# The MLPs of a two-layer diffusion backbone: chunks of 1024 in layer 0, seven quarter products with all weight sums on VectorE in layer 1

## The chip, the cores and the metric

The kernel runs on one core of one Trainium2 chip. TensorE multiplies matrices into PSUM (which this kernel uses as eight banks of 128 partitions by 512 fp32 columns), VectorE and ScalarE work element by element, GpSimd and SyncE here mostly issue transfers. The metric is the device time of one execution in microseconds; of the kernel before, three were timed.

## The reference, cut to what matters

Everything is fp32. There are two layers over 512 latent tokens and 256 context tokens, width 1024, hidden width of the MLP 4096. In layer 0 both token sets run through the MLP, in layer 1 only the latent tokens.

```python
def sq_relu_mlp(h, w1, w2):
    return jnp.square(jax.nn.relu(h @ w1)) @ w2

for l in range(DEPTH):                      # DEPTH = 2
    ...                                     # modulation, token mixer
    x = x + g1 * ox
    x = x + g2 * sq_relu_mlp(modulate(rmsnorm(x, norm_mlp[l]), sh2, sc2), w_ff1[l], w_ff2[l])
    if not last:
        h = h + cg1 * oc
        h = h + cg2 * sq_relu_mlp(modulate(rmsnorm(h, norm_mlp[l]), csh2, csc2), w_ff1[l], w_ff2[l])
return rmsnorm(x, norm_final)
```

The modulation (shift, scale, gate) comes from `silu(c) @ w_ada[l] + b_ada[l]`.

## The kernel before

Activations lie transposed: a tile holds 128 channels by the tokens (512 in layer 1, 512 + 256 = 768 in layer 0). Each fp32 operand is split into a rounded high part and the remainder, and each product of 128 x 128 weights is three matmuls (`mm3`: high x high, high x low, low x high). Weights arrive from HBM in tiles of up to 1024 columns (`load_unit`), and `split_piece` makes pieces of 512 columns out of them: ScalarE copies with rounding (`hi`, L219), VectorE subtracts (`lo`, L228).

The program is a list of tasks in order, one task about one output tile. `emit` walks through it; ahead of each task it splits weights up to AP_ = 4 pieces beyond the one needed, holds at most N_W = 6 split pieces, and loads units as long as at most N_R = 4 raw tiles are in use. `merge` mixes two lists in proportion to their costs. From this the recording layer makes one queue for each engine, which the engine works off in that order; an instruction that waits holds up what stands behind it on its engine.

Layer 0 MLP (`layer_ff` with `last` false): 8 chunks of 512 hidden channels. An "up" task makes a hidden tile in two halves of 384 tokens, each in a single PSUM bank; `evac` does the ReLU and the square on ScalarE and splits the result. Then eight "down" outputs (`plain`) sum over the chunk's four hidden tiles in a two-bank tile (512 + 256 columns), and VectorE adds them, times the gate, to x (`gate_update`, L1257). Between these tasks 96 tasks of row products for the modulation of layer 1 (L488, VectorE alone) are spread over the first seven chunks.

Layer 1 MLP (`last` true): 4 chunks of 1024. In the first three, the down product is taken as 2 x 2 blocks and computed with seven quarter products instead of eight (`block`, `product`): the weight quarters A11, A12, A22, A21 and their sums S1 to S4, against sums of the hidden tiles. S1 and S3 are formed by transfers: one brings a quarter twice (L240), another, issued by GpSimd, adds two further quarters to it (L244, accumulating). S2 and S4 are formed by VectorE (L264). Each product is 12 matmuls of 256 columns. What is shared between outputs is kept in tiles called V (`keep`, L1376, the first time copied by ScalarE, L1469), the rest goes straight to x (`gate`, L1461); `finish` combines the kept sums at the end. The fourth chunk is plain. All single banks are taken in a rotation over three two-bank tiles and two single banks (`bank`).

The last outputs of a layer run one token group after another (256 tokens each), so that the next norm (sum of squares, `norm_h` L565 to L569) can begin on the first groups.

Of the kernel before, what the change touches and what calls it, by code (L numbers as in the profile page):

```python
# [52 lines left out]
TAIL1 = 2  # L53
TL = False
# [8 lines left out]
N_RR = 2  # L63
# [27 lines left out]
class Unit:  # L91
# [4 lines left out]

    def __init__(self, ap, w, kind=None, queue=None):
        self.ap, self.w, self.kind, self.queue, self.plain = ap, w, kind, queue, False
# [49 lines left out]
class Net:  # L148
    def __init__(self, nc, tc, es, a):
# [9 lines left out]
        self.ps = self.half = None  # L159
        self.turn = 0  # L160
# [4 lines left out]
    def psum(self, na, nb):  # L165
# [4 lines left out]
        self.pa = self.ps.enter_context(self.tc.tile_pool(name=self.nm("pa"), bufs=na, space=PSUM))  # L170
# [499 lines left out]
    def layer_mix(self, l):  # L670
# [580 lines left out]
        out.append(Task(0, lambda: self.psum(3, 2)))  # L1251
# [9 lines left out]
    def residual_tasks(self, l, units, rhs, nk, chunk, whole, groups, tail, then=None):  # L1261
# [11 lines left out]
        def go(m, gs):  # L1273
            ps = self.A("res")
# [3 lines left out]
        def two(gs):  # L1278
            ps = [self.A("res"), self.A("res")]
# [52 lines left out]
    def layer_ff(self, l, whole, groups):  # L1332


# [4 lines left out]
        last = l == DEPTH - 1  # L1339
        w = NL if last else T  # L1340
        hw = w // 2
        MP = 1 if last else 2
        CP = 4 // MP
        n_chunk, n_blk = 16 // CP, 4 // MP
        halves = [[(0, 256, 0)], [(256, 256, 0)]] if last else [[(0, 384, 0)], [(384, 128, 0), (512, 256, 1)]]
        H = lambda k: self.h[k]
        out = []
        then = self.final_tasks(groups) if last else self.norm_tasks(l + 1, self.G1, 0, groups)
        B11, T1, B21, B22, T3, T2, T4 = range(7)
        act, st = {}, {}  # L1350
        per = T // hw
# [13 lines left out]
        def begin():  # L1365
            n = per * 2 // 4
            t = [self.d("V", F32).rearrange("p a t -> p (a t)") for _ in range(-(-3 // n))]
            for i, name in enumerate("U57"):
                st[name] = [t[i // n][:, (i % n * 4 + j) * hw:(i % n * 4 + j + 1) * hw] for j in range(4)]

        def negate():
            self.ng = self.sm.tile([P, 8, 2], F32, tag="ng", name=self.nm("ng"), bufs=1)
            w = 1 if last else 2
            nc.vector.tensor_scalar(self.ng[:, :, :w], self.mod[l][:, 40:48, :w], -1.0, None, op0=ALU.mult)
# [4 lines left out]
        def split_plain(c, m, half):  # L1379
            if (c, m) not in act:  # L1380
                t = self.d("act").rearrange("p a t -> p (a t)") if not last or m % 3 != 2 else None
                if not last:
                    act[c, m] = Halves(t[:, 0:T], t[:, T:2 * T])
                elif t is not None:
                    act[c, m] = Halves(t[:, 0:512], t[:, 512:1024])
                    act["spare", m] = t[:, 1024:1536]
                else:
                    act[c, m] = Halves(act.pop(("spare", m - 2)), act.pop(("spare", m - 1)))
            f = act[c, m]
            s = slice(0, w) if half is None else slice(half * hw, half * hw + hw)  # L1390
            b = st["b", m % 2][:, s]
            self.hi(f[:, 0, s], b)
            self.mark = self.lo(f[:, 1, s], b, f[:, 0, s])
# [22 lines left out]
        def evac(c, m, half, parts):  # L1416

            if half in (0, None):
                st["b", m % 2] = self.tmp("b")
            b = st["b", m % 2]  # L1420
            for ps, at, n in parts:
                nc.scalar.activation(b[:, at:at + n], ps, AF.Relu)  # L1422
            o, n = (0, w) if half is None else (half * hw, hw)
            nc.scalar.activation(b[:, o:o + n], b[:, o:o + n], AF.Square)
            if not last or c == n_chunk - 1:
                split_plain(c, m, half)
                return
            for i in (0, 1) if half is None else (half,):
                sums(c, m, i)

        def up(c, m, u):
            for half in (None,) if last else range(2):
                o, n = (half * hw, hw) if half is not None else (0, w)
                ps = self.bank("f1")
                for k in range(NK):
                    s = slice(k * P, (k + 1) * P)
                    self.mm3(ps[:, :n], u[:, 0, s], u[:, 1, s], H(k)[:, 0, o:o + n], H(k)[:, 1, o:o + n], k == 0, k == NK - 1)
                evac(c, m, half, [(ps[:, :n], o, n)])

        def up_two(us):  # L1440

            ps = [self.A("f1") for _ in us]
# [6 lines left out]
            for i in range(2):  # L1449
                for half in range(2):  # L1450
                    o = half * hw
                    evac(0, i, half, [(ps[i][:, o:o + hw], o, hw)])

        def gate(m, half, ps, neg=False):

            g = self.ng[:, m] if neg else self.mod[l][:, 40 + m]
            o = half * hw
            self.mark = None
            for at, n, cond in halves[half]:
                x = self.X(m)[:, at:at + n]  # L1460
                self.mark = nc.vector.scalar_tensor_tensor(x, ps[:, at - o:at - o + n], g[:, cond:cond + 1], x,  # L1461
# [292 lines left out]
```

## Time and profile before

| what | value |
|---|---|
| median of 3 runs | 1622.08 us (1621.45 to 1624.95) |
| the profiled execution | 1622.75 us, of which 1620.9 are its span |
| mean granted TensorE clock | 0.987 |
| TensorE (PE) busy | 1561.1 us, 96% of the span |
| weight loads (PEld) busy | 1334.8 us, 82%, beside PE |
| VectorE (DVE) busy | 1011.6 us, 62% |
| ScalarE (ACT) busy | 749.6 us, 46% |
| GpSimd (POOL) busy | 48.5 us, 3% |

The MLP of layer 0 runs from about 405 to 970 us, that of layer 1 from about 1250 us to the end. "Busy" says that an instruction was running; matmuls are pipelined and their ends are modelled. The granted clock is given as a share of 2.4 GHz. In a timeline, a number in brackets is the engine's idle time before that work, and behind the arrow stands what the profile takes to have ended it. In the chain of waits the last instruction of the program is followed back, step by step, to what released it.

### The profile page before, as it was taken

Reading aid. Unit: us, or ns where it says so; the run is one execution under the profiler, and the core shown is the slowest. Engines: PE = TensorE matmul, PEld = TensorE weight load, DVE = VectorE, ACT = ScalarE, POOL = GpSimd, SP = SyncE. Lnnn points to the kernel's source line nnn. Section 1 sums busy time; section 2 is a strip of 40 time slices with the busy share of each in tenths; the row PEclk is TensorE's granted clock in tenths of the full one; section 3 lists DMA queues with packets and bytes.
Section 4 is the critical chain, followed back from the end, with each engine's and each line's share of the span. In section 5 each row is a group of like instructions: output and inputs, shape, how many; then the busy total and the mean of one; then the engine's idle time right before and its main releaser. Section 6 shows DMA issues by size and latency. Waiting matters only on the chain.

```text
span 1620.9 us, 24503 instructions
## 1 busy us (share of the span) xinstructions
PE 1561.1 (96%) x9268; PEld 1334.8 (82%) x9268; DVE 1011.6 (62%) x2234; ACT 749.6 (46%) x1545; POOL 48.5 (3%) x90
## 2 busy tenths in 40 slices
PE   4999999999999999999999989999999999999997
PEld 2898657888889899898998988867888888888886
DVE  5665664886867655445454377686646775758734
ACT  4425466653524232242322454367754645445443
POOL 0110000000000000000000001101000000000000
PEclk8999999999999999999999999999999999999999
DMA  9352344554254334333333133524323354445421
GB/s 376 105 170 66 116 120 106 164 185 150 90 158 156 117 106 128 118 117 117 111 106 122 66 112 121 153 82 103 96 88 116 103 150 124 130 129 130 126 85 53
DMA packets 76966, 201.42 MB, mean 124 GB/s; under 512 B 9648, under 2 KB 12208, under 8 KB 76848
## 3 DMA queue, kind: packets, MB, share of 16 engines
q1 hardware_dynamic: 71728, 183.33, 36.0%
q0 software_dynamic: 4544, 16.00, 5.0%
q8 instruction: 73, 1.20, 0.3%
q10 hardware_dynamic: 576, 0.52, 0.1%
q14 instruction: 45, 0.37, 0.1%
HBM read 169.40 MB, written 10.49 MB: 111 GB/s over the span
## 4 chain that ended last, share of the span: by engine, by line
PE 88%; DVE 5%; DMA 4%; ACT 2%; issue 1%; SPq 0%; DVEq 0%; ACTq 0%
PE f L211 52%; PE A L211 10%; PE sc L211 4%; PE oe L211 3%; PE pv L211 3%; PE res L211 3%; PE rv L211 2%; PE pT L1045 2%; PE ada L211 2%; DMA sums<-w_ff 1%; PE ro L211 1%; PE q L211 1%; DMA raw<-w_ada 1%; PE rs L211 1%; DVE hn L565 1%
## 5 line engine op out<-in xcount | busy, mean ns | idle before, releaser
L211 PE MATMUL f<-h,wt 128*128 128x384 f32 (+2 forms) x2400 | 458.3, 351 | 2.6 <-ACT h L568 1.7
L211 PE MATMUL f<-act,wt 128*128 128x256 f32 (+1 forms) x2832 | 448.8, 319 | 7.0 <-DVE x L1461 4.4
L211 PEld LDWEIGHTS f<-h,wt 128*128 128x128 f32 x2400 | 412.5, 189 | 47.0 <-ACT b L1422 6.8
L211 PEld LDWEIGHTS f<-act,wt 128*128 128x128 f32 x2832 | 400.7, 190 | 53.5 <-DVE x L1461 5.2
L228 DVE TENSOR_TENSOR wt<-raw,wt 128x512 fp32r<-128x512 f32 (+1 forms) x320 | 218.5, 688 | 207.4 <-ACT wt L219 203.3
L219 ACT ACTIVATE wt<-raw 128x512 fp32r<-128x512 f32 (+1 forms) x320 | 199.2, 629 | 308.7 <-PE f L211 203.1
L211 PE MATMUL A<-h,wt 128*128 128x512 f32 (+2 forms) x864 | 172.3, 358 | 1.0 <-ACT h L568 0.5
L211 PEld LDWEIGHTS A<-h,wt 128*128 128x128 f32 x864 | 143.6, 191 | 27.3 <-ACT h L568 2.8
L1422 ACT ACTIVATE b<-f 128x384 f32<-128x384 f32 (+2 forms) x98 | 50.2, 518 | 158.2 <-PE f L211 158.1
L1257 DVE SCALAR_TENSOR_TENSOR x<-f,mod,x 128x256 f32<-128x256 f32 (+1 forms) x142 | 80.9, 602 | 55.4 <-PE f L211 55.4
L228 DVE TENSOR_TENSOR act<-b,act 128x384 fp32r<-128x384 f32 (+2 forms) x108 | 55.1, 521 | 71.0 <-ACT act L219 70.9
L211 PE MATMUL sc<-k,q 96*128 96x512 f32 (+1 forms) x384 | 85.5, 351 | 4.1 <-ACT p L1027 3.3
L488 DVE SCALAR_TENSOR_TENSOR rows<-rows,sbc 128x512 f32<-128x512 f32 x128 | 86.9, 685 | 1.8 <-DMA rows<-w_adaT 0.9
L211 PEld LDWEIGHTS sc<-k,q 96*128 96x128 f32 x384 | 63.2, 189 | 20.3 <-ACT p L1027 6.1
L1026 DVE TENSOR_REDUCE st<-sc 128x1 f32<-128x768 f32 x64 | 60.7, 952 | 15.5 <-PE sc L211 15.2
L1046 ACT ACTIVATE pT<-pT 128x384 f32<-128x384 f32 x128 | 56.8, 491 | 23.2 <-PE pT L1045 22.6
L219 ACT ACTIVATE wt<-sums 128x512 fp32r<-128x512 f32 x44 | 27.5, 625 | 86.3 <-PE f L211 82.5
L211 PE MATMUL res<-mix,wt 128*128 128x256 f32 (+1 forms) x384 | 59.1, 313 | 2.3 <-DVE om L1066 1.9
L1027 ACT ACTIVATE p<-sc,st 128x768 f32<-128x768 f32 x64 | 57.8, 903 | 6.1 <-DVE st L1026 4.8
L211 PE MATMUL oe<-mix,wt 128*128 128x512 f32 (+1 forms) x288 | 60.4, 363 | 0.0
L211 PEld LDWEIGHTS res<-mix,wt 128*128 128x128 f32 x384 | 53.1, 189 | 8.2 <-DVE om L1066 2.8
L211 PEld LDWEIGHTS oe<-mix,wt 128*128 128x128 f32 x288 | 47.5, 189 | 10.3 <-issue 1.5
(246 smaller groups left out, 1655.1 us busy)
## 6 DMA issues: line engine op xcount, KB each, us to landing
raw<-w_ff SPq DMA_DIRECT2D x96, 512.0 KB, 3.7
rows<-w_adaT SPq DMA_DIRECT2D x128, 256.0 KB, 2.8
raw<-w_in SPq DMA_DIRECT2D x22, 512.0 KB, 4.3
raw<-w_ada SPq DMA_DIRECT2D x16, 512.0 KB, 10.7
rows<-w_ada SPq DMA_DIRECT2D x32, 256.0 KB, 3.2
raw<-w_ff SPq DMA_DIRECT2D x32, 256.0 KB, 3.1
raw<-w_out SPq DMA_DIRECT2D x16, 512.0 KB, 3.7
sums<-w_ff SPq DMA_DIRECT2D x12, 512.0 KB, 4.0
```

The source lines that it names most:

```text
L211: self.nc.tensor.matmul(out, l, r, start=start, stop=stop)
L219: self.nc.scalar.activation(out, src, AF.Copy, **k)
L228: return self.nc.vector.tensor_tensor(out, src, hi.bitcast(F32), op=ALU.subtract)
L488: nc.vector.scalar_tensor_tensor(out, w, 1.0, self.sbc[:, v, half], op0=ALU.mult, op1=ALU.mult, accum_out=acc[:, v, i, j:j + 1])
L565: nc.vector.scalar_tensor_tensor(t[:, :n], self.X(k)[:, o:o + n], G, self.ss[:, 1, o:o + n], op0=ALU.mult, op1=ALU.mult)
L1026: nc.vector.tensor_reduce(st[:, 0:1], ps, axis=AX, op=ALU.max, negate=True)
L1027: nc.scalar.activation(p, ps, AF.Exp, bias=st[:, 0:1], accum_out=st[:, 1:2])
L1045: nc.tensor.transpose(ps[:, kt, :], p[:, (k0 + kt) * P:(k0 + kt + 1) * P], self.ident)
L1046: nc.scalar.activation(s["pT", h, qt // 2][:, k0:k0 + 3, c], ps, AF.Copy)
L1257: self.gated = self.gated[-1:] + [self.nc.vector.scalar_tensor_tensor(x, ps[:, o:o + n], self.mod[l][:, chunk * 8 + k, cond:cond + 1], x, ...
L1422: nc.scalar.activation(b[:, at:at + n], ps, AF.Relu)
```

## The change

In layer 0, four chunks of 1024 replace eight of 512. An up tile is one two-bank tile of 768 columns; ScalarE does the ReLU, VectorE multiplies it by the PSUM tile, which gives the square. The down outputs sum over eight hidden tiles, with the same function as the output projection (`residual_tasks`), whose first two outputs run six of eight terms before the last two hidden tiles are touched. The 96 row tasks are spread over the MLP by cost (FT), and three row buffers stand in place of two (N_RR). In layer 1, all four weight sums are formed by VectorE from two plain loads; the eight PSUM banks are one pool of single banks. The matmuls stay the same in number. In the rest of `layer_ff_last` the branches for layer 0 are gone, and the old code for layer 1 stands otherwise.

```diff
+FT = -36
-N_RR = 2
+N_RR = 3
...
+    def R(self, l):
+
+        return self.B([P, NL], "res") if l == DEPTH - 1 else self.A("res")
...
         if u.kind == "st":
-            u.raw = [self.wr.tile([P, UW], F32, tag="r", name=self.nm(n)) for n in ("sums", "raw")]
-            u.raw.append(self.wr.tile([P, 512], F32, tag="rh", name=self.nm("raw"), bufs=2))
-            r = u.raw[0].rearrange("p (a c) -> p a c", a=2)
-            if u.plain:
-                q.dma_start(r[:, 0, :], u.ap[:, 0:512])
-            else:
-                q.dma_start(r, u.ap[:, None, 0:512].to_broadcast([P, 2, 512]))
-            q.dma_start(u.raw[1], u.ap[:, 1024:2048])
-            q.dma_start(u.raw[2], u.ap[:, 512:1024])
-            if not u.plain:
-                self.nc.gpsimd.dma_start(u.raw[0], u.ap[:, 512:1536], accum_op=ALU.add)
+            u.raw = [self.wr.tile([P, UW], F32, tag="r", name=self.nm("raw")) for _ in range(2)]
+            for i in range(2):
+                q.dma_start(u.raw[i], u.ap[:, i * 1024:i * 1024 + 1024])
             return
...
-        if i not in (S2, S4):
-            t, o = {A21: (0, 0), S1: (0, 0), S3: (0, 1), A11: (1, 0), A12: (1, 1), A22: (2, 0)}[i]
-            return u.raw[t][:, o * 512:o * 512 + 512]
+        if i < 4:
+            return u.raw[i // 2][:, i % 2 * 512:i % 2 * 512 + 512]
         if i not in u.sums:
-            a, b = {S2: (S1, A11), S4: (S2, A12)}[i]
+            a, b = {S1: (A21, A22), S2: (S1, A11), S3: (A11, A21), S4: (S2, A12)}[i]
             a, b = self.quarter(u, a), self.quarter(u, b)
             t = u.sums[i] = self.tmp("sum")[:, 0:512]
             self.nc.vector.tensor_tensor(t, a, b, op=ALU.add)
...
-        out.append(Task(0, lambda: self.psum(3, 2)))
+        out.append(Task(0, lambda: self.psum(3, 2) if l < DEPTH - 1 else self.psum(0, 8)))
...
+        def evac(c, m, ps):
+            t = self.d("ra", F32)
+            nc.scalar.activation(t[:, 0, :w], ps[:, :w], AF.Relu)
+            nc.vector.tensor_tensor(t[:, 1, :w], t[:, 0, :w], ps[:, :w], op=ALU.mult)
+            f = act[c, m] = self.d("act")
+            self.hi(f[:, 0, :w], t[:, 1, :w])
+            self.mark = self.lo(f[:, 1, :w], t[:, 1, :w], f[:, 0, :w])
+
+        for c in range(N_CHUNK):
+            u1 = [Unit(a["w_ff1"][l, 8 * c + m], 1024) for m in range(8)]
+            u2 = [Unit(a["w_ff2"][l, c, m], 1024) for m in range(8)]
...
+            for m in range(m0, 8):
+                out.append(self.lin_task(u1[m], H, gs, lambda ps, c=c, m=m: evac(c, m, ps)))
+            end = c == N_CHUNK - 1
+            out += self.residual_tasks(l, u2, lambda k, c=c: act[c, k], NK, 5, whole, groups,
+                                       TAIL1 if end else 0, then if end else None)
+        return out
+
+    def layer_ff_last(self, l, groups):
...
+        def product(c, u, j, name):
             q, f = use[name]
-            ps = self.bank("f2")[:, :hw]
+            ps = self.B([P, 512], "f2")[:, :hw]
             t = u.pieces[name].t
             for p in range(CP):
...
+        def block(c, j, u):
+            return [Task(3 * CP * hw / 2.2, lambda n=n: product(c, u, j, n), (u.pieces[n],))
+                    for n in (A11, S1, A12, S4, S3, S2, A22)]
...
+            blocks = [Unit(a["w_ff2q"][0, c * n_blk + j], 2048, "st") for j in range(n_blk)]
             if c < n_chunk - 1:
...
+                for j in range(n_blk):
+                    out += block(c, j, blocks[j])
...
-            ff = self.layer_ff(l, whole, groups)
-            tasks += ff
+            ff = self.layer_ff(l, whole, groups) if l < DEPTH - 1 else self.layer_ff_last(l, groups)
+            if l == DEPTH - 1:
+                tasks += ff
+                continue
+            e = self.extra
+            tasks += merge(ff[:7], e.pop(("ff1", l), [])) + merge(ff[7:FT], e.pop(("ff", l), [])) + ff[FT:]
```

How it moves the queues is seen at three places. First VectorE in layer 1, in the third down stage, within one block: `wt` is a split of a weight piece, `sum` a weight sum, `V` a kept sum, `x` a gated update, `f` a product in PSUM. Before:

```order
L228 TENSOR_TENSOR wt_14311<-sums_14093,wt_14311 128x512
L1376 TENSOR_TENSOR V_12021<-V_12021,f_2290_14314 128x256
L1461 SCALAR_TENSOR_TENSOR x_1909_11688<-f_2287_14281,mod_156,x_1909_11688 128x256
L228 TENSOR_TENSOR wt_14328<-raw_14094,wt_14328 128x512
L1376 TENSOR_TENSOR V_12019<-V_12019,f_2292_14331 128x256
L264 TENSOR_TENSOR sum_14345<-sums_14093,raw_14094 128x512
L1376 TENSOR_TENSOR V_12021<-V_12021,V_12019 128x256
L264 TENSOR_TENSOR sum_14347<-sum_14345,raw_14094 128x512
L264 TENSOR_TENSOR sum_14473<-sums_14274,raw_14275 128x512
L1461 SCALAR_TENSOR_TENSOR x_1909_11688<-f_2292_14331,ng_12458,x_1909_11688 128x256
L228 TENSOR_TENSOR wt_14349<-sum_14347,wt_14349 128x512
L228 TENSOR_TENSOR wt_14365<-sums_14093,wt_14365 128x512
```

After, the same place:

```order
L221 TENSOR_TENSOR wt_14042<-raw_13840,wt_14042 128x512
L1457 SCALAR_TENSOR_TENSOR x_1845_11407<-f_2261_14045,mod_156,x_1845_11407 128x256
L248 TENSOR_TENSOR sum_14059<-raw_13841 128x512
L1396 TENSOR_TENSOR V_11882<-V_11882,f_2264_14064 128x256
L1396 TENSOR_TENSOR V_11881<-V_11881,f_2266_14081 128x256
L221 TENSOR_TENSOR wt_14061<-sum_14059,wt_14061 128x512
L221 TENSOR_TENSOR wt_14078<-raw_13840,wt_14078 128x512
L248 TENSOR_TENSOR sum_14095<-sum_14059,raw_13840 128x512
L1457 SCALAR_TENSOR_TENSOR x_1845_11407<-f_2270_14102,ng_11883,x_1845_11407 128x256
L248 TENSOR_TENSOR sum_14097<-sum_14095,raw_13840 128x512
L248 TENSOR_TENSOR sum_14116<-raw_13840,raw_13841 128x512
L1396 TENSOR_TENSOR V_11881<-V_11881,f_2273_14121 128x256
```

The weight sums now come from `raw` tiles alone, and there are four to a block; the combination of kept sums (V from two V) that stood among them before stands behind the last product now.

Second, TensorE in layer 0, where one kind of task turns into the other. Before, down (`act`) to up (`h`):

```order
L211 MATMUL f_928_4987<-act_4467,wt_4801 128x256 x3
L211 MATMUL f_928_4987<-act_4551,wt_4801 128x256 x3
L211 MATMUL f_928_4987<-act_4477,wt_4804 128x256 x3
L211 MATMUL f_928_4987<-act_4636,wt_4804 128x256 x3
L211 MATMUL f_935_5030<-h_763_4024,wt_4860 128x384 x3
L211 MATMUL f_935_5030<-h_764_4025,wt_4860 128x384 x3
L211 MATMUL f_935_5030<-h_765_4026,wt_4860 128x384 x3
L211 MATMUL f_935_5030<-h_766_4027,wt_4860 128x384 x3
```

After, up to down:

```order
L204 MATMUL A_4858<-h_768_4029,wt_4703 128x512 x3
L204 MATMUL A_4858<-h_768_4029,wt_4703 128x256 x3
L204 MATMUL A_4858<-h_769_4030,wt_4703 128x512 x3
L204 MATMUL A_4858<-h_769_4030,wt_4703 128x256 x3
L204 MATMUL A_4858<-h_770_4031,wt_4703 128x512 x3
L204 MATMUL A_4858<-h_770_4031,wt_4703 128x256 x3
L204 MATMUL res_4936<-act_4455,wt_4773 128x512 x3
L204 MATMUL res_4936<-act_4455,wt_4773 128x256 x3
L204 MATMUL res_4936<-act_4461,wt_4773 128x512 x3
```

An up tile alternates between 512 and 256 columns where it had 384, and a down output (`res`) walks through its hidden tiles with both widths at each.

Third, VectorE at the seam of the layers: `ss` sums up squares, `nv` and `nq` belong to the norm's root, `hn` and `h` are the normed tile, `x` an update of the last outputs. Before, between the first and the second token group:

```order
L538 TENSOR_TENSOR ss_8736<-ss_8736,sq_9086 128x256
L548 TENSOR_SCALAR nv_9092<-ssum_9089 128x256
L1257 SCALAR_TENSOR_TENSOR x_731_3781<-f_1408_9108,mod_155,x_731_3781 128x256
L551 SCALAR_TENSOR_TENSOR nq_9093<-nv_9092,nq_9093 128x256
L1257 SCALAR_TENSOR_TENSOR x_732_3782<-f_1412_9133,mod_155,x_732_3782 128x256
L552 SCALAR_TENSOR_TENSOR ss_8736<-nq_9093,ss_8736 128x256
L228 TENSOR_TENSOR wt_9150<-raw_8675,wt_9150 128x512
L565 SCALAR_TENSOR_TENSOR hn_9100<-x_729_3779,G_1_158,ss_8736 128x256
L565 SCALAR_TENSOR_TENSOR hn_9104<-x_729_3779,G_1_158,ss_8736 128x256
L565 SCALAR_TENSOR_TENSOR hn_9125<-x_730_3780,G_1_158,ss_8736 128x256
L538 TENSOR_TENSOR ss_8736<-ss_8736,sq_9122 128x256
L569 SCALAR_TENSOR_TENSOR h_1376_8971<-hn_9100,mod_156,h_1376_8971 128x256
```

After:

```order
L522 TENSOR_TENSOR ss_8215<-ss_8215,sq_8830 128x256
L532 TENSOR_SCALAR nv_8844<-ssum_8841 128x256
L1241 SCALAR_TENSOR_TENSOR x_732_3782<-res_8868,mod_155,x_732_3782 128x256
L535 SCALAR_TENSOR_TENSOR nq_8845<-nv_8844,nq_8845 128x256
L221 TENSOR_TENSOR wt_8969<-raw_8572,wt_8969 128x512
L536 SCALAR_TENSOR_TENSOR ss_8215<-nq_8845,ss_8215 128x256
L221 TENSOR_TENSOR wt_8972<-raw_8572,wt_8972 128x512
L549 SCALAR_TENSOR_TENSOR hn_8852<-x_729_3779,G_1_158,ss_8215 128x256
L549 SCALAR_TENSOR_TENSOR hn_8856<-x_729_3779,G_1_158,ss_8215 128x256
L549 SCALAR_TENSOR_TENSOR hn_8860<-x_730_3780,G_1_158,ss_8215 128x256
L553 SCALAR_TENSOR_TENSOR h_1321_8725<-hn_8852,mod_156,h_1321_8725 128x256
```

One update and one addition of squares fewer stand there, and one weight split more.

## Rows read from the trace of the kernel before

**Rows 1.** The page, first part: each engine's busy time, share and instructions.
```profile
PE 1561.1 (96%) x9268; PEld 1334.8 (82%) x9268; DVE 1011.6 (62%) x2234; ACT 749.6 (46%) x1545; POOL 48.5 (3%) x90
```

**Rows 2.** Windows: busy time and count by engine, granted clock, DMA share.
```profile
core 0: us, PE busy (x) PEld busy (x) DVE busy (x) ACT busy (x) POOL busy (x), PEclk, DMA share, GB/s
470.00:955.00 485.00, 485.00 (x2775) 447.69 (x2775) 261.78 (x596) 157.03 (x295) 0.00 (x0) 1.00 0.38 119
955.00:980.00 25.00, 17.89 (x114) 16.17 (x113) 23.05 (x58) 15.93 (x38) 0.00 (x0) 0.86 0.23 88
1296.81:1344.53 47.72, 43.92 (x340) 42.30 (x339) 33.53 (x63) 23.03 (x48) 1.74 (x2) 0.96 0.52 144
1389.79:1433.52 43.73, 41.31 (x332) 40.72 (x330) 34.48 (x72) 18.20 (x35) 1.74 (x2) 0.96 0.53 147
1478.54:1520.01 41.47, 41.22 (x341) 40.65 (x340) 40.57 (x87) 19.42 (x36) 1.74 (x2) 1.00 0.59 166
1324.00:1328.00 4.00, 4.00 (x24) 4.00 (x24) 2.22 (x4) 2.11 (x5) 0.00 (x0) 0.63 0.37 124
```

**Rows 3.** Timeline of PE, layer 1 MLP: start, length, work, idle before it.
```profile
1322.37 20.14 PE L211 MATMUL f<-act,wt 128*128 128x256 f32 x149 [3.77 <-DVE x L1461]
...
1414.30 1.09 PE L211 MATMUL f<-act,wt 128*128 128x256 f32 x7 [1.79 <-DVE wt L228]
...
1416.02 17.67 PE L211 MATMUL f<-act,wt 128*128 128x256 f32 x135 [0.63 <-DVE x L1461]
...
1433.52 45.19 PE L211 MATMUL f<-h,wt 128*128 128x512 f32 x192
```

**Rows 4.** Chain that ended last: start, length, what.
```profile
1311.04 7.91 DMA sums<-w_ff
...
1405.79 6.41 DMA sums<-w_ff
```

**Rows 5.** DMA issues: tile, queue, count, KB each, median us to landing.
```profile
raw<-w_ff SPq DMA_DIRECT2D x96, 512.0 KB, 3.7
...
sums<-w_ff SPq DMA_DIRECT2D x12, 512.0 KB, 4.0
...
sums<-w_ff POOLq DMA_DIRECT2D x12, 512.0 KB, 6.3
```

**Rows 6.** Timeline of DVE near the end of the third down stage.
```profile
1516.72 0.75 DVE L1376 TENSOR_TENSOR V<-V,V 128x256 f32<-128x256 f32 x2
...
1518.19 1.29 DVE L228 TENSOR_TENSOR wt<-raw,wt 128x512 fp32r<-128x512 f32 x2
1519.40 0.48 DVE L1461 SCALAR_TENSOR_TENSOR x<-V,mod,x 128x256 f32<-128x256 f32 x1
1519.80 0.48 DVE L1461 SCALAR_TENSOR_TENSOR x<-V,ng,x 128x256 f32<-128x256 f32 x1
```

**Rows 7.** Timeline of PE, one chunk of the layer 0 MLP.
```profile
593.48 33.42 PE L211 MATMUL f<-act,wt 128*128 128x512 f32 x189
626.73 29.62 PE L211 MATMUL f<-h,wt 128*128 128x384 f32 x168
```

**Rows 8.** Groups by line and shape: busy us, mean ns; idle before, releaser.
```profile
L219 ACT ACTIVATE wt<-raw 128x512 fp32r<-128x512 f32 x310 | 193.0, 629 | 303.9 <-PE f L211 203.1 <-PE oe L211 33.5 <-PE A L211 31.2
...
L1257 DVE SCALAR_TENSOR_TENSOR x<-f,mod,x 128x512 f32<-128x512 f32 x66 | 49.4, 748 | 50.3 <-PE f L211 50.3
...
L228 DVE TENSOR_TENSOR act<-b,act 128x384 fp32r<-128x384 f32 x64 | 35.4, 557 | 67.0 <-ACT act L219 67.0
...
L551 DVE SCALAR_TENSOR_TENSOR nq<-nv,nq 128x768 f32<-128x768 f32 x5 | 4.8, 956 | 3.5 <-ACT nq L550 3.5
```

**Rows 9.** Timeline of PE where layer 0 ends and layer 1 begins.
```profile
965.56 2.81 PE L211 MATMUL f<-act,wt 128*128 128x256 f32 x20
...
974.56 1.22 PE L211 MATMUL ssum<-ss,one 128*128 128x256 f32 x2 [6.19 <-DVE ss L538]
```

**Rows 10.** Waits of PE in the layer 0 mixer (160 to 375 us).
```profile
PE ada L211 <- DMA rows<-w_ada: 2.3, 2, 1.6
```

More of the change, by code (lines that the diff above doesn't have):

```diff
@@ L97, in __init__ @@
     def __init__(self, ap, w, kind=None, queue=None):
-        self.ap, self.w, self.kind, self.queue, self.plain = ap, w, kind, queue, False
+        self.ap, self.w, self.kind, self.queue = ap, w, kind, queue
         self.raw, self.sums = None, {}
@@ L158, in __init__ @@
         self.dp = pool("dp", N_DP)
-        self.ps = self.half = None
-        self.turn = 0
+        self.ps = None
         self.es = es
@@ L1338, in layer_ff @@
         nc, a = self.nc, self.a
[L1339 to L1345, printed above, removed]
+        gs = [(0, NL), (NL, NC)]
+        w = T
         H = lambda k: self.h[k]
         out = []
-        then = self.final_tasks(groups) if last else self.norm_tasks(l + 1, self.G1, 0, groups)
+        then = self.norm_tasks(l + 1, self.G1, 0, groups)
@@ L1349, in layer_ff @@
+        return out
+    def layer_ff_last(self, l, groups):
+        nc, a = self.nc, self.a
+        w, hw, CP, n_chunk, n_blk, per = NL, NL // 2, 4, 4, 4, 2 * T // NL
+        H = lambda k: self.h[k]
+        whole = [(0, NL, 0)]
+        out = []
+        then = self.final_tasks(groups)
         B11, T1, B21, B22, T3, T2, T4 = range(7)
         act, st = {}, {}
-        per = T // hw
         def part(c, p, q):
@@ L1365, in begin @@
         def begin():
-            n = per * 2 // 4
-            t = [self.d("V", F32).rearrange("p a t -> p (a t)") for _ in range(-(-3 // n))]
+            t = [self.d("V", F32).rearrange("p a t -> p (a t)") for _ in range(2)]
             for i, name in enumerate("U57"):
[L1369 to L1374, printed above, removed]
+                at = [4 * i + j for j in range(4)]
+                st[name] = [t[x // 6][:, x % 6 * hw:x % 6 * hw + hw] for x in at]
@@ L1376, in layer_ff @@
+            self.ng = self.sm.tile([P, 8], F32, tag="ng", name=self.nm("ng"), bufs=1)
+            nc.vector.tensor_scalar(self.ng, self.mod[l][:, 40:48, 0], -1.0, None, op0=ALU.mult)
         add = lambda x, y, z, op=ALU.add: nc.vector.tensor_tensor(x, y, z, op=op)
         neg = lambda x, y, z: nc.vector.scalar_tensor_tensor(x, y, -1.0, z, op0=ALU.mult, op1=ALU.subtract)
[L1379 to L1388, printed above, removed]
-            f = act[c, m]
[L1390 to L1393, printed above, removed]
@@ L1414, in sums @@
             put(c, p, T4, v[:, hw:w])
[L1416 to L1429, printed above, removed]
-        def up(c, m, u):
[L1432 to L1438, printed above, removed]
+        def up(c, m, u):
+            ps = self.B([P, 512], "f1")
+            self.lin1(ps, u, H, NK, 0, w)
+            evac(c, m, ps)
         def up_two(us):
-            ps = [self.A("f1") for _ in us]
+            ps = [self.B([P, 512], "f1") for _ in us]
             for o, n, _ in groups:
@@ L1529, in layer_ff @@
-        spread = self.extra.pop(("ff", l), [])
+            return [Task(cost, lambda odd=odd: plain(c, u, j, odd, gs),
+                         tuple(u.pieces[n] for n in ((A21, A22) if odd else (A11, A12)))) for odd in range(2)]
+        cost = self.lin_cost(NK, [(0, w)])
         for c in range(n_chunk):
-            us = [Unit(a["w_ff1"][l, 2 * CP * c + m], 1024) for m in range(2 * CP)]
+            us = [Unit(a["w_ff1"][l, 8 * c + m], 1024) for m in range(8)]
             m0, ups = 0, []
-            cost = self.lin_cost(NK, [(0, hw)] * 2)
@@ L1544, in layer_ff @@
                 ups = merge(ups, [Task(1, lambda j=j: finish(j)) for j in range(4)])
-            blocks = [Unit(a["w_ff2"][l, c * n_blk + blk], 2048, "st") for blk in range(n_blk)]
-            for u in blocks:
-                u.plain = not last or c == n_chunk - 1
-            downs = []
+            out += ups
+            blocks = [Unit(a["w_ff2q"][0, c * n_blk + j], 2048, "st") for j in range(n_blk)]
             if c < n_chunk - 1:
-                for blk in range(n_blk):
-                    downs += block(c, blk, blocks[blk]) if last else plain_tasks(c, blocks[blk], blk, whole)
@@ L1552, in layer_ff @@
-            share = -(-len(spread) // max(n_chunk - 1 - c, 1))
-            extra, spread = spread[:share], spread[share:]
-            if c == 0:
-                out += merge(ups, self.extra.pop(("ff1", l), []))
-                out += merge(downs, extra)
-            else:
-                out += merge(ups + downs, extra)
+                for j in range(n_blk):
+                    out += block(c, j, blocks[j])
         out.append(Task(0, self.stat_start))
-        for blk in range(n_blk - 1):
-            out += plain_tasks(c, blocks[blk], blk, whole)
+        for j in range(n_blk - 1):
+            out += plain_tasks(c, blocks[j], j, whole)
```

116 lines of the change are left out of this document (60 added, 56 removed).

## The prediction

> **What bounds the kernel now.** I read the page first: TensorE is busy for 96% of the span, VectorE for 62%, ScalarE for 46% [rows 1]. So what the change does to another engine counts only where TensorE stops for it. Next the windows by stage [rows 2]: in the layer 0 MLP, 470 to 955 us, TensorE has no idle time at all, at a granted clock of 1.00. At the seam of the two layers it is idle for 7.1 of 25 us. In layer 1 the MLP has three "down" stages with seven quarter products. Each is 336 matmuls of 256 columns (7 products x 4 blocks x 12), the same work three times, yet they take 47.72, 43.73 and 41.47 us. They need trimming to be compared, because the queue lets a few matmuls of a neighbour in: the first holds 3 of the next up stage, the third 4, at 0.234 us each (45.19 us for 192 [rows 3]), and the second lacks 6 of its own, done earlier, at 0.12 us. That gives 47.0, 44.4 and 40.5 us, so the first two lose 10.4 us together against the third.
>
> The timeline tells where: TensorE stands still for 3.77 us in the first, 1.79 and 0.63 us in the second [rows 3], and afterwards runs slowly: from 1324 to 1328 us the mean granted clock is 0.63, a mix of the 2.4 and the 1.2 GHz level [rows 2]. The chain of waits names the cause, "DMA sums<-w_ff", three times in these two stages (two shown, 7.91 and 6.41 us) [rows 4]: the weight sums S1 and S3 are made by a transfer that adds to what a first transfer brought. The first lands 4.0 us after issue, the adding one, which GpSimd can issue only then, 6.3 us after its own; a plain 512 KB transfer takes 3.7 us [rows 5]. The releaser printed at the gap is VectorE, but VectorE had itself waited for the sums.
>
> **Layer 1: the sums move to VectorE.** Per block the two chained transfers go, and S1 and S3 become two additions of 512 columns, 24 in the twelve blocks. The additions must fit between what VectorE does. From starts in a row [rows 6]: two 512-column subtractions take 1.29 us and the second alone 0.69, so they follow each other at 0.60 us; 256-column additions at 0.33; gated updates at 0.40 (1519.40 to 1519.80). Before, a block costs 9 x 0.60 (7 splits, 2 sums) + 4 x 0.33 + 4 x 0.40 = 8.3 us; after, 11 x 0.60 + 2.9 = 9.5 us. In the first stage three of the four additions are copies on ScalarE, so 8.5. TensorE needs 40.5 / 4 = 10.1 us for a block. VectorE thus goes to 94% of TensorE's pace and still does not set it. The trace holds a proof that such a load can be carried: in the third stage VectorE is busy for 40.57 of 41.47 us [rows 2], because the closing combination of the stored sums (6 additions, 6 updates, 4.4 us) was queued there, and TensorE loses next to nothing. In the changed order those closing operations stand behind the last product, while 6 more sums (3.6 us) come in: a little less load than that stage bore already.
>
> What is late next is the start of a down stage. The queue puts the sum S3 between the last hidden tile's operations, and its split behind an addition and an update of the first product. That is 0.60 + 0.33 + 0.40 = 1.3 us of VectorE ahead of a split which the fifth product (5.7 us in) waits for. I charge 0.6 us per stage, half of it, since product five's first two thirds need only ScalarE's half of the split. The plain loads are not late: a block's buffers come free when its own splits are done, and they are wanted a block, about 10 us, later, against 3.7 us to land. All three stages at 40.5 + 0.6 = 41.1 us: 5.9 + 3.3 - 0.6 = **8.6 us gained**. The best is 10.4 us (no charge). The lower bound takes VectorE's operations at their full durations (0.69, 0.42, 0.48): 11 x 0.69 + 4 x 0.42 + 4 x 0.48 = 11.2 us a block, 45.4 us with the charge in stages two and three, which leaves 5.9 - 1.0 - 4.9 = 0 us.
>
> The eight single banks change little: before, the rotation of whole and half tiles also gave these products eight banks in turn. GpSimd's 12 issues vanish from an engine that is 3% busy [rows 1].
>
> **Layer 0: plain chunks of 1024.** The number of matmuls stays. Up tiles go from 384 + 384 to 512 + 256 columns, 1440 matmuls changing shape. In one chunk 168 of the first kind take 29.62 us, 176.3 ns each, and 189 of the second mix 33.42, 176.8 ns [rows 7]; with equal parts of 512 (0.234) and 256 (0.1195, the third stage's 40.5 / 336 less its own waits) it would be 177. So 0.5 to 1.3 ns x 1440: 0.7 to 1.9 us, taken as **1.2 us lost**. ScalarE's squares become VectorE products out of PSUM, 8 per chunk of 768 columns, between 0.956 us (such an operation from SBUF) and 1.12 (the 0.748 of a 512-column update out of PSUM, scaled) [rows 8]: 7.6 to 9.0 us. Against that a sum over eight tiles instead of four halves the updates (8 x (0.748 + 0.48) = 9.8 us less) and eight splits of 768 replace sixteen of 384 (8 x 0.956 against 16 x 0.557: 1.3 us less). VectorE, 261.78 of 485 us busy there [rows 2], gains some air. All of this lies under TensorE's 485 us; if the cover went, it would be the 9 us per chunk, 36 in all. A two-bank tile is wanted again two tiles (2 x 48 x 0.177 = 17 us) later, against two operations of about 1 us that empty it. At the turn from up to down, the first two outputs run six of their eight terms before they touch the last two hidden tiles: 72 x 0.177 = 12.7 us of cover.
>
> **The seam.** TensorE waits 6.19 us for VectorE's sum of squares [rows 9], and VectorE is busy for 23.05 of 25 us [rows 2], so here VectorE sets the end. The last block had four outputs in three token groups; now it is two. From the first norm to the last value of the second group, three updates (0.40) and four additions (0.33) fall away, 2.5 us, but two weight splits (1.2) come ahead of it. Taken as **1.3 us gained**, bounds 0 and 2.5.
>
> **The mixer of layer 0.** A third row buffer lets the adaLN rows load earlier; TensorE waited 2.3 us for them [rows 10]. The order around them shifts too, so between 2.3 gained and 2.3 lost. I take **0.5 us gained**, nearest to a wait that only partly goes.
>
> **Sum.** -8.6 + 1.2 - 1.3 - 0.5 = -9.2 us. The profiled execution took 1622.75 us, of which 1.85 lie outside its span; it stands 0.67 above the median of the runs, 1622.08. 1622.75 - 9.2 = 1613.55 for such an execution, and 1612.9 for a median. The times below are medians.
>
> **Rivals.** *VectorE keeps the old pace of stage two.* If its operations did not overlap, the down stages give nothing (the lower bound) and the rest is 1.2 - 1.3 - 0.5 = -0.6: 1621.5. Against it stand the starts 0.60 us apart in [rows 6]; for it, that dependent sums in a row might not overlap so. The Trainium skill, page "VectorE: DVE Perf Modes", section "The DRAIN you can't avoid", says that the next operation does not start until the pipeline is empty, and adds that one which is not held starts earlier; by its first clause this rival would be the forecast, and the trace agrees with the second.
>
> *The hand-off to ScalarE decides (slower).* Each sum is added on VectorE, rounded on ScalarE, subtracted on VectorE. If the queue stood still for each of the four round trips, one ScalarE operation of 0.629 us each [rows 8], a block would take 9.5 + 2.5 = 12.0 us instead of 10.1. Three stages of 48.0 against 47.0, 44.4 and 40.5 are 12.1 us lost, with the rest 11.5: 1633.6. It turns slower than before where a block takes more than 11.0 us: then twelve blocks cost 132 us, as much as now. For it: sums stand close before their splits. Against: an update or another sum stands between in the order, and stage three ran so already.
>
> *The loads stay late.* If the plain loads made TensorE wait as the sums did, because buffers come free late, the 8.6 us are not gained: 1621.5. Against it: no second transfer waits for a first any more.
>
> **How the numbers follow.** The forecast has 0.78, its own range 1607.6 to 1617: the best of each term (-10.4 + 0.7 - 2.5 - 2.3 = -14.5) gives 1607.6, half of the stages' gain (4.3) with the rest 1617. No overlap has 0.07, late loads 0.06, the hand-off 0.09. Less than 0.2% (3.2 us) can't be told from no change here, so below 1618.8 is faster: that is the forecast, 0.78. The two middle rivals are the same, 0.13, and the hand-off is slower, 0.09. The range 1607 to 1622 takes in the forecast and the middle rivals; the hand-off lies outside.
>
> **What would show it.** Right: three down stages of about 41 us each, no gap there above 1 us, clock at 1.00, VectorE over 90% busy in them; layer 0 MLP without idle time and 1 to 2 us longer; the wait at the seam near 5 us. Wrong: stages two and three longer than 43 us with VectorE as releaser (no overlap), with ScalarE's weight copies as releaser (hand-off), or with a load as releaser. A layer 0 MLP with idle TensorE would break the largest cover I rely on.

## The result and the profile after

The changed kernel took 1599.54 us (median of four, 1597.23 to 1601.0), the kernel before 1622.54 beside it: a ratio of 0.9855, interval 0.9838 to 0.9872. The gain of some 23 us has the sign that was forecast and two and a half times the size. The profiled execution took 1597.23 us, 25.5 less than that of before. The page's first part [rows 1]:

```profile
PE 1546.6 (97%) x9268; PEld 1303.0 (82%) x9268; DVE 1009.1 (63%) x2189; ACT 710.6 (45%) x1411; POOL 38.0 (2%) x78
```

The same 9268 matmuls are 14.5 us shorter on TensorE, and 11 us of idle time are gone. The three down stages of layer 1 by windows and the first by the timeline [rows 2, 3]:

```profile
core 0: us, PE busy (x) PEld busy (x) DVE busy (x) ACT busy (x) POOL busy (x), PEclk, DMA share, GB/s
1283.55:1323.52 39.97, 39.96 (x337) 39.61 (x336) 36.05 (x69) 23.03 (x48) 0.00 (x0) 1.00 0.40 119
1368.50:1408.78 40.28, 40.24 (x338) 40.00 (x337) 38.45 (x80) 19.46 (x36) 0.00 (x0) 1.00 0.37 106
1453.75:1493.82 40.07, 39.98 (x338) 39.66 (x337) 38.11 (x79) 19.39 (x36) 0.00 (x0) 1.00 0.35 106
```

```profile
1283.55 40.13 PE L204 MATMUL f<-act,wt 128*128 128x256 f32 x336
1323.52 1.80 PE L204 MATMUL f<-h,wt 128*128 128x512 f32 x7
```

Each stage is now 336 matmuls in one piece, at the full clock. Then the seam of the layers [rows 9] and the waits in layer 0's mixer from 160 us to its output [rows 10]:

```profile
958.90 0.70 PE L204 MATMUL ssum<-ss,one 128*128 128x256 f32 x2 [1.88 <-DVE ss L522]
962.43 1.98 PE L204 MATMUL A<-h,wt 128*128 128x384 f32 x5 [2.83 <-ACT h L552]
```

```profile
PE sc L204 <- ACT p L1011: 1.0, 3, 0.5
PE ada L204 <- DMA rows<-w_ada: 0.7, 1, 0.7
PE pTc L1078 <- ACT p L1068: 0.4, 1, 0.4
```

Points that both programs have (a first product of a part, in TensorE's timeline) divide the 25.5 us:

| part of the program | before, us | after, us | difference | forecast |
|---|---|---|---|---|
| start, up to the first `qr` | 168.7 | 166.4 | -2.2 | 0 |
| layer 0 mixer, up to its output | 206.7 | 199.8 | -7.0 | -0.5 |
| layer 0 output | 37.2 | 37.2 | 0 | 0 |
| layer 0 MLP and seam, up to the first `rx` | 582.5 | 579.3 | -3.2 | +1.2 - 1.3 |
| layer 1 mixer | 227.6 | 226.5 | -1.1 | 0 |
| layer 1 output, up to its MLP | 34.1 | 34.3 | +0.3 | 0 |
| layer 1 MLP | 354.9 | 342.9 | -12.0 | -8.6 |
| tail | 9.2 | 8.9 | -0.2 | 0 |

Not all of it belongs to the change. In the thirteen profiles of this study, which do the same work at the start, the first part took 166.2 to 169.3 us; the granted clock from 40 to 60 us was 0.91 before and 1.00 after. The layer 1 mixer took 226.5 to 227.8. So about 3 us of this pair of profiles are chance.

### The profile page after: what moved, and what is told of

Its sections match the earlier page's. It is cut to its first block, busy times and chain, and to the rows that moved or that the text cites. A ratio compares the mean times of both kernels' runs of the same rounds, so it can differ in the third digit from the quotient of the medians.

```text
span 1595.4 us, 24146 instructions
## 1 busy us (share of the span) xinstructions
PE 1546.6 (97%) x9268; PEld 1303.0 (82%) x9268; DVE 1009.1 (63%) x2189; ACT 710.6 (45%) x1411; POOL 38.0 (2%) x78
## 4 chain that ended last, share of the span: by engine, by line
PE 91%; DVE 4%; DMA 2%; ACT 2%; issue 1%; SPq 0%; DVEq 0%; ACTq 0%
PE A L204 27%; PE f L204 21%; PE res L204 19%; PE sc L204 4%; PE oe L204 3%; PE pv L204 3%; PE rv L204 2%; PE pT L1029 2%; PE ada L204 2%; PE ro L204 1%; PE q L204 1%; DMA raw<-w_ada 1%; DVE hn L549 1%; DMA raw<-w_in 1%; PE rs L204 1%; PE v L204 1%
## 5 line engine op out<-in xcount | busy, mean ns | idle before, releaser
L204 PE MATMUL A<-h,wt 128*128 128x512 f32 (+2 forms) x2448 | 446.8, 342 | 4.1 <-ACT h L552 2.8
L204 PEld LDWEIGHTS A<-h,wt 128*128 128x128 f32 x2448 | 382.4, 189 | 67.5 <-ACT h L552 5.1
L204 PE MATMUL res<-act,wt 128*128 128x256 f32 (+1 forms) x1584 | 272.8, 334 | 0.0
L204 PEld LDWEIGHTS res<-act,wt 128*128 128x128 f32 x1584 | 239.2, 189 | 33.0
L204 PE MATMUL f<-h,wt 128*128 128x512 f32 (+1 forms) x816 | 181.9, 384 | 1.0 <-ACT h L552 1.0
L204 PEld LDWEIGHTS f<-h,wt 128*128 128x128 f32 x816 | 147.0, 188 | 34.4 <-ACT h L552 1.4
L204 PE MATMUL f<-act,wt 128*128 128x256 f32 (+1 forms) x1248 | 166.2, 294 | 0.1
L204 PEld LDWEIGHTS f<-act,wt 128*128 128x128 f32 x1248 | 158.4, 188 | 8.1 <-DVE wt L221 0.5
L1241 DVE SCALAR_TENSOR_TENSOR x<-res,mod,x 128x512 f32<-128x512 f32 (+1 forms) x98 | 54.2, 583 | 88.7 <-PE res L204 88.6
L1329 DVE TENSOR_TENSOR ra<-ra,A 128x768 f32<-128x768 f32 x32 | 30.5, 954 | 92.6 <-ACT ra L1328 92.6
```

The lines of the kernel that those rows point to most:

```text
L204: self.nc.tensor.matmul(out, l, r, start=start, stop=stop)
L1241: self.gated = self.gated[-1:] + [self.nc.vector.scalar_tensor_tensor(x, ps[:, o:o + n], self.mod[l][:, chunk * 8 + k, cond:cond + 1], x, ...
L1329: nc.vector.tensor_tensor(t[:, 1, :w], t[:, 0, :w], ps[:, :w], op=ALU.mult)
```

## Experiments

Two questions: what evened out the down stages, the sums on VectorE or the banks; and what shortened the mixer. Ratios are to runs of the kernel before on the same chip. First each part by itself.

**Sums on VectorE in the kernel before, alone, and with the third row buffer:**

```diff
-                q.dma_start(r, u.ap[:, None, 0:512].to_broadcast([P, 2, 512]))
...
-                self.nc.gpsimd.dma_start(u.raw[0], u.ap[:, 512:1536], accum_op=ALU.add)
+            for i in range(2):
+                q.dma_start(u.raw[i], u.ap[:, i * 1024:i * 1024 + 1024])
...
+            a, b = {S1: (A21, A22), S2: (S1, A11), S3: (A11, A21), S4: (S2, A12)}[i]
```

The second kernel has `N_RR = 3` besides.

> The kernel before with layer 1's four weight sums on VectorE from two plain loads, and nothing else. Theory: the three down stages take 40 to 41 us each, no idle time of TensorE above 1 us in them, and the whole is 11 to 12 us shorter: 1611. Prediction's term: 8.6 us, 1614. Rival (the pool of eight single banks was what made the stages even): stages two and three stay above 43 us, 1617 or more.

> The kernel before with layer 1's sums on VectorE (two plain loads of 1024 columns) and three row buffers in place of two; layer 0's MLP stays as before. Theory (the third row buffer shortens layer 0's mixer by about 7 us, since the row products of the modulation, 32 contraction rows each, then stand next to each other on TensorE and cost one visit of 0.98 us for up to six of them, and takes two such visits out of layer 0's MLP): 1622.5 - 11.6 (down stages) - 7 - 2 = about 1602, with 22 visits in place of 27. Rival (the mixer's gain comes from the new order of the MLP or from the larger descriptor memory, not from the row buffers): as the kernel with the sums alone, about 1611, and 27 visits.

The sums alone: 1619.54 us, 0.9984 (0.9975 to 0.9992), about 2.6 us where 8.6 were forecast, and a layer 1 MLP of 353.8 us. The theory fell. Its first down stage:

```profile
1297.49 3.15 PE L211 MATMUL f<-act,wt 128*128 128x256 f32 x24
1302.74 38.62 PE L211 MATMUL f<-act,wt 128*128 128x256 f32 x300 [2.10 <-ACT wt L219]
```

After 24 matmuls, two products, TensorE stands for a weight split. The listing of TensorE's queue names the split: it is S3's. In the kernel before the products of the first block stand as A11, A12, S3, S2, the next block's A11, and only then S1, S4 and A22, which lie in the second halves of two-bank tiles; here, too, A11 and A12 are followed by S3. By the listing, every product in a second half (32 in the three stages, in either kernel) waits until the first half of its tile has been read. With eight single banks the products stand as written: A11, S1, A12, S4, S3, S2, A22. The prediction compared only VectorE's queue here.

The three stages by windows:

```profile
1297.49:1343.39 45.90, 43.78 (x340) 42.21 (x339) 37.41 (x70) 23.56 (x48) 0.00 (x0) 0.96 0.34 104
1388.84:1429.44 40.60, 39.12 (x330) 38.67 (x328) 38.93 (x80) 19.18 (x36) 0.00 (x0) 1.00 0.35 113
1474.47:1519.79 45.32, 43.20 (x342) 42.48 (x341) 42.28 (x87) 19.66 (x36) 0.00 (x0) 0.96 0.35 107
```

Against 47.72, 43.73 and 41.47 us [rows 2] the sums shorten the first two stages and lengthen the third by 3.9 us: it begins with the same 24 matmuls and the same 2.10 us as the first.

With the third row buffer 1612.36 us, 0.9932 (0.9918 to 0.9946), 7.2 us less; layer 0's mixer took 199.4 us in place of 205.7. The miss against 1602 is that of the sums. By TensorE's queue the visits of row products fell from 25 to 21, not from 27 to 22.

**Layer 0's chunks alone, and the whole change with two row buffers** (`N_RR = 2`):

> The kernel before with layer 0's MLP in plain chunks of 1024 and its spread of the row tasks, two row buffers, layer 1 untouched. Theory: +1.0 us for the tile shapes (a chunk of 1024 took 135.68 us after against twice 67.71 before), -2.4 us at the seam: 1621, and layer 0's mixer starts its output projection at 375 us as before. Rival (the new list of tasks also reorders the mixer, and the gain of 7 us there comes with it): 1614, output projection at 368 us or earlier.

> The changed kernel with two row buffers in place of three. Theory (the row buffer carries the mixer's gain): 9 us slower than the changed kernel, 1608.5, output projection of layer 0 at 373 to 375 us, 25 or more visits of row products. Rival (the row buffer carries at most the 0.5 to 2.3 us that the prediction gave it): 1600 to 1602.

Chunks alone: 1618.8 us, 0.9974 (0.9963 to 0.9986), some 4 us where 1.4 were expected; layer 0's MLP and seam took 579.1 us, the mixer 205.3 as without them. Two row buffers: 1605.52 us, 0.9889 (0.9876 to 0.9903), 6 us over the changed kernel; mixer 205.2. The row buffer carries the mixer's gain, 5.4 to 6.3 of the 7 us. The larger descriptor memory of the changed kernel does not: with two row buffers it is there and the mixer does not gain, and the kernel with the sums and three row buffers gains without it. The waits with two row buffers, against those above:

```profile
PE sc L204 <- ACT p L1011: 1.8, 2, 1.1
PE ada L204 <- DMA rows<-w_ada: 1.3, 1, 1.3
PE adaT L204 <- ACT rows L431: 0.7, 1, 0.7
PE rvar L906 <- ACT op L899: 0.4, 1, 0.4
PE pTc L1078 <- ACT p L1068: 0.4, 1, 0.4
```

TensorE's whole idle time there was 5.6 us with two buffers and 3.4 with three. Most of the rest is in the visits of the row products (`ada`). Changed kernel, TensorE:

```profile
186.13 1.05 PE L204 MATMUL ada<-rows,sc 128*32 128x512 f32 x4
187.12 1.08 PE L204 MATMUL ro<-P,V 128*64 128x256 f32 x8
...
192.72 1.06 PE L204 MATMUL ada<-rows,sc 128*32 128x512 f32 x6
193.71 0.65 PE L204 MATMUL ro<-P,V 128*64 128x256 f32 x2
...
198.93 1.04 PE L204 MATMUL ada<-rows,sc 128*32 128x512 f32 x2
199.91 0.44 PE L204 MATMUL ro<-P,V 128*64 128x256 f32 x2
```

Here two, four or six of them cost 0.98 to 0.99 us until the next work starts; a visit of four can also be two pairs one behind the other (1.85 us at 215.38 us in the kernel before). With rows there earlier, more stand together: 15 visits in the mixer in place of 18, which take 15.8 us of TensorE in place of 18.1.

**Banks and sums crossed.** The changed kernel with two row buffers and the accumulating transfers; and, in the kernel before, the banks alone:

```diff
-        out.append(Task(0, lambda: self.psum(3, 2)))
+        out.append(Task(0, lambda: self.psum(3, 2) if l < DEPTH - 1 else self.psum(0, 8)))
...
     def bank(self, name):
+        if self.pa is None:
+            return self.B([P, 512], name)
```

> The changed kernel with two row buffers, eight single banks, but S1 and S3 formed by the accumulating transfers as before. It completes a square: the sums alone on VectorE (kernel before) took 1619.5 and its layer 1 MLP only 1.1 us less than before, both together (changed kernel, two row buffers) 1605.5 and 12.0 us less. Theory (the banks decide: in the rotation of two-bank tiles TensorE's queue holds the product with S3 at the third place of a stage, with single banks at the fifth, 2.9 us later): gaps of 3.8 and 2.4 us shrink to about 1 and 0, the layer 1 MLP is 9 us shorter than before, 1608. Rival (the two chained transfers are late whatever the order, so both parts are needed): stages one and two keep 47 and 44 us, 1614 to 1616.

> The kernel before with one pool of eight single banks in layer 1's MLP in place of the rotation over three two-bank tiles and two single banks; sums by accumulating transfers, layer 0 and row buffers as before. Theory (the banks alone even out the down stages, because TensorE's queue then holds the products in their own order, that with S3 fifth): layer 1's MLP 341 to 342 us in place of 353 to 356, the whole 13 us shorter: 1609. Rival (the accumulating transfers keep stages one and two above 43 us unless layer 0 is changed too): 1617 or more.

The first took 1603.97 us, 0.9888 (0.9872 to 0.9905), as much as with sums on VectorE (0.9889); the banks alone 1609.94, 0.9928 (0.991 to 0.9946). Banks alone, the down stages:

```profile
1296.55:1336.29 39.74, 39.74 (x337) 39.65 (x336) 31.29 (x62) 23.06 (x47) 1.74 (x2) 1.00 0.60 169
1381.27:1420.69 39.42, 39.42 (x337) 39.42 (x336) 34.93 (x74) 19.14 (x35) 1.74 (x2) 1.00 0.59 171
1465.68:1505.39 39.71, 39.71 (x337) 39.66 (x336) 34.88 (x76) 19.03 (x35) 1.75 (x2) 1.00 0.56 157
```

Not a gap, with transfers as before. They still land late: in the three stages VectorE waits for them longer than in the kernel before (first line: before, second: banks alone), and TensorE no longer waits at all.

```profile
DVE sum L264 <- DMA sums<-w_ff: 7.9, 3, 4.3
DVE sum L268 <- DMA sums<-w_ff: 11.6, 4, 4.8
```

How that wait reached TensorE in the kernel before, its traces show, TensorE first and VectorE below:

```profile
1296.81 21.79 PE L211 MATMUL f<-act,wt 128*128 128x256 f32 x175
...
1478.54 14.97 PE L211 MATMUL f<-act,wt 128*128 128x256 f32 x124
```

```profile
1318.97 0.69 DVE L264 TENSOR_TENSOR sum<-sums,raw 128x512 f32<-128x512 f32 x1 [4.26 <-DMA sums<-w_ff]
...
1321.84 0.47 DVE L1461 SCALAR_TENSOR_TENSOR x<-f,ng,x 128x256 f32<-128x256 f32 x1
```

The gap of 3.77 us [rows 3] comes after 175 matmuls, not at S3's product. By the listing, what waits there is the third block's A11. It lies in the second half of the tile that holds the second block's A22, so it waits for the update that reads A22 (at 1321.84), and this update stood on VectorE behind a sum that had waited 4.26 us for its transfer. The 0.63 us of the second stage are a wait of the same kind, the 1.79 us one for the split of S4, which stood behind such a sum too. The third stage, with S3's product third as in the first, runs 124 matmuls before a first short gap. So with the transfers the late sums reached TensorE mostly through the shared tiles, and with the sums on VectorE through the place of S3's product; single banks take away both. No run separates the two in the kernel with transfers.

The layer 1 MLP by kernel: old banks 354.9, 356.6 (chunks alone), 353.8 and 353.3 (sums on VectorE); single banks 341.3 and 341.8 with transfers, 342.9 with sums on VectorE (two row buffers and three). The banks are worth 11 to 15 us; the sums on VectorE give nothing beside them.

**S3's product put back to the third place, nothing else:**

```diff
-            return [Task(3 * CP * hw / 2.2, lambda n=n: product(c, u, j, n), (u.pieces[n],))
-                    for n in (A11, S1, A12, S4, S3, S2, A22)]
+            need = {S3: (A12, S4, S3)}
+            return [Task(3 * CP * hw / 2.2, lambda n=n: product(c, u, j, n), tuple(u.pieces[x] for x in need.get(n, (n,))))
+                    for n in (A11, S1, S3, A12, S4, S2, A22)]
```

> The changed kernel with the product that uses S3 moved from the fifth to the third place of each block on TensorE; the order of splits and sums on VectorE through the first S3 stays. Theory (what the two-bank rotation cost was the place of S3's product: its split is ready 4.8 us after a stage's start, the third place comes at 2.9): a wait of about 2 us at the start of each down stage, as in the kernel with the sums alone, and a lower clock behind it: 3 x 3.3 = 10 us slower, about 1610. Rival (the two-bank tiles cost by being held longer, not by the order): within 1.5 us of the changed kernel, 1598 to 1601.

1611.79 us, 0.9938 (0.9922 to 0.9954), 12 to 13 us over the changed kernel (0.9855), 10 forecast. The first stage, by timeline and windows:

```profile
1286.79 2.97 PE L204 MATMUL f<-act,wt 128*128 128x256 f32 x24
1292.29 7.94 PE L204 MATMUL f<-act,wt 128*128 128x256 f32 x52 [2.52 <-ACT wt L212]
```

```profile
1286.79:1289.79 3.00, 2.98 (x25) 2.77 (x23) 1.50 (x5) 2.58 (x6) 0.00 (x0) 1.00 0.00 0
1289.79:1292.29 2.50, 0.00 (x0) 0.00 (x1) 2.50 (x7) 1.53 (x5) 0.00 (x0) 1.00 0.00 0
1292.29:1297.00 4.71, 4.71 (x27) 4.71 (x28) 3.67 (x7) 2.73 (x6) 0.00 (x0) 0.66 0.66 189
...
1286.79:1330.92 44.13, 41.61 (x337) 41.40 (x336) 37.25 (x69) 23.98 (x48) 0.00 (x0) 0.96 0.36 109
```

The same 24 matmuls as with the sums alone, and a gap of 2.5 us where it was 2.1. It costs twice: 2.5 us of standing, and 0.34 x 4.71 = 1.6 us at the lower clock behind it, together the 4.2 us by which the stage is longer than the changed kernel's 39.97. So with the sums on VectorE the place in the queue alone costs as much as the two-bank tiles do, and the lower clock follows the stand. It does not speak for the kernel before, whose gaps stand elsewhere.

**How near VectorE is to its limit:** S1 and S3 each added twice (`for _ in range(2 if i in (S1, S3) else 1):` ahead of the addition).

> The changed kernel in which VectorE forms S1 and S3 twice (the same addition again, 24 additions of 512 columns more, results unchanged). Theory (the prediction's pace: 9.5 us of VectorE a block at starts 0.60 us apart, TensorE 10.1): 10.7 us a block, so stages two and three grow by 4 x 0.6 = 2.5 us each, stage one (8.5 + 1.2 = 9.7 us a block) does not: 5 us slower than the changed kernel, 1604.5. Rival one (VectorE has more room than the sum of starts says): 1600. Rival two (full durations, 0.69 an addition, VectorE at its limit already): 24 x 0.69 = 16.6 us slower, 1616.

1604.78 us, 0.99 (0.9883 to 0.9917). Stages two and three:

```profile
1373.80:1417.20 43.40, 42.93 (x337) 40.60 (x336) 41.96 (x86) 19.34 (x36) 0.00 (x0) 1.00 0.30 94
1462.20:1505.70 43.50, 43.01 (x338) 40.63 (x336) 42.07 (x86) 19.33 (x36) 0.00 (x0) 1.00 0.30 94
```

43.4 us where 4 x 10.7 = 42.8 were worked out, and stage one 40.9. The layer 1 MLP grew by 7.5 us (350.4, in the profiled execution, at 1609.23 us the slowest of four), nearer to the 5 of the pace by starts than to the 16.6 of full durations. The Trainium skill's first clause (page "VectorE: DVE Perf Modes", section "The DRAIN you can't avoid"), by which an operation waits until the pipeline is empty, would have given the latter; the trace again agrees with its second.

**Versions that might have been better,** as changes to the changed kernel; in the first two the sums come by the accumulating transfers again:

```diff
+            u.raw.append(self.wr.tile([P, 512], F32, tag="rh", name=self.nm("raw"), bufs=1))   # first
...
+N_RR = 5; N_DP = 21              # second
...
+AU = 2; N_RR = 6; N_DP = 21      # third
```

> The changed kernel with S1 and S3 formed by the accumulating transfers as before (one buffer for the quarter A22 in place of two, to make room), three row buffers, eight single banks. Theory (with single banks, 24 additions more on VectorE cost 0.5 us a stage and gain nothing): 1.6 us less than the changed kernel, 1598. Rival (the transfers' waits on VectorE, or the single buffer for A22, cost TensorE something): 1600 or more.

> As the kernel with single banks and accumulating transfers, but with five row buffers (one working tile of 6 KB fewer) and both buffers for A22. Theory (fewer visits of row products only help as long as ScalarE and VectorE are not the next to be waited for, which they were at 9 visits in layer 0's mixer): 17 visits on the queue in place of 21, half of the 4 us gained: 2 us less than with three row buffers, 1596. Rival (the mixer is already at that limit): 1598.

> The changed kernel with row tasks of four row products in place of two (AU = 2), six row buffers, and one working tile of 6 KB fewer to make room (N_DP = 21). Theory (a visit of row products costs TensorE 0.98 us whether it holds two, four or six of them): TensorE's queue has 12 visits in place of 21, so 9 x 0.98 = 8.8 us less than the changed kernel: 1590.7. Rival (tasks of four wait for their four loads, or the smaller working pool delays others): the waits for rows grow by as much as the visits shrink, 1599 or more.

They took 1597.6 us (0.9857, 0.9837 to 0.9876), 1599.77 (0.9866, 0.9847 to 0.9886) and 1600.6 (0.9865, 0.985 to 0.9879): none can be told from the changed kernel. The third nearly halves the visits in the mixer, 9 in place of 15, and the mixer still takes 200.8 us against 199.8. Its waits:

```profile
PE sc L204 <- ACT p L1011: 3.0, 3, 1.3
PE ro L204 <- DVE P L859: 2.2, 1, 2.2
PE pT L1029 <- DVE q L968: 1.2, 2, 0.7
PE sc L204 <- ACT op L898: 0.9, 1, 0.9
```

TensorE's busy time there fell from 196.4 to 191.8 us, its idle time rose from 3.4 to 9.0: what the visits give, waits for ScalarE and VectorE take. With five buffers the mixer took 202.7 us, 6.6 of them idle.

## Why the prediction was wrong

- **The step that failed: "The eight single banks change little".** The prediction took the halves of a two-bank tile for banks of their own and put the gain of the down stages down to the sums. The crossed kernels show the reverse: banks alone, 13 us of the layer 1 MLP; sums alone, 1 us of it. The late transfers were real, and with single banks VectorE still waits 11.6 us for them; they made TensorE wait because a product in a second half has to wait until VectorE has read the first. With the sums on VectorE the same tiles put S3's product third, ahead of its split, and the third stage lost 3.9 us. That the total came near (8.6 forecast, 12.0 measured) was luck.
- **"I take 0.5 us gained", the mixer of layer 0,** was the largest miss in size: 5 to 6 us by the row buffer. The bounds of 2.3 us held only the wait for rows. The visits (three fewer, 2.3 us) and the waits of other products that went with them (for ScalarE, 1.9 us by the two lists above) were left out; the price of a visit could have been read in the trace of before.
- **Layer 0's tile shapes: right for the up tiles, not for the whole stretch.** A chunk of 1024 takes 135.68 us now; before, half as much work took 67.73, from 593.48 [rows 7] to the next such place:

```profile
661.21 33.42 PE L211 MATMUL f<-act,wt 128*128 128x512 f32 x189
```

```profile
547.96 68.00 PE L204 MATMUL A<-h,wt 128*128 128x512 f32 x384
615.80 68.00 PE L204 MATMUL res<-act,wt 128*128 128x512 f32 x384
683.64 68.00 PE L204 MATMUL A<-h,wt 128*128 128x512 f32 x384
```

  That is 0.2 us a chunk, the sum of two changes. Over the whole stretch, from start to start and without the waits, the up matmuls took 1.8 us more (272.9 in place of 271.1; 0.7 to 1.9 forecast), and the down matmuls 1.9 us less (272.0 in place of 273.9), which was not forecast and whose cause is open. Apart from the seam the stretch got 2.2 us shorter where the prediction had it 1 to 2 us longer: visits of row products (six in place of seven, 1.2 us) and short waits (0.7 us) are the rest.
- **The seam: right within its bounds.** TensorE waits 1.88 + 2.83 = 4.7 us (5 forecast); from the MLP's end to the next product it takes 5.4 us in place of 7.9, 2.4 us gained against 1.3 (0 to 2.5).
- **VectorE's pace: right.** 38.45 of 40.28 us busy, no overload. The charge of 0.6 us a stage was right too, only against another base: with transfers a stage takes 39.6 us, with the sums 40.1. The third stage of before, taken as undisturbed at 40.5, was not.
- **The rivals** of VectorE without overlap, of late loads and of the hand-off to ScalarE did not come: no gap is left in the stages.

## What to carry to other kernels

Count the order on the engine that waits, not only the number of buffers: halves of one two-bank tile are not two banks to the queue. A product in the second half waited for the reading of the first, and a product moved from the fifth place of a block to the third cost 12 to 13 us. A wait that a releaser explains has two ends; ask which of them the change moves. And cross the parts of a change before crediting one: here the part with the most new code did nothing.

## What the runs showed of the hardware

Row products with 32 output partitions cost TensorE 0.98 us a visit in most visits, whether two, four or six stand together; a visit of four as two pairs in a row cost 1.85 us. A stand of 2.5 us was followed by 4.7 us at a mean granted clock of 0.66, whereas stands of 0.3 to 0.4 us with VectorE at its limit left it at 1.00, and so did one of 1.25 us in the second stage of the kernel with the sums alone. The first 169 us of programs with the same start differ by up to 3 us.
